# Modulation vectors on GpSimd alone, in buffers of their own, spread over the scans

## The chip, the core and the metric

The kernel runs on one core of one Trainium2 chip. The metric is the device time of one execution in microseconds (us). The engines are called as in the profile: PE (TensorE; PEld is its weight load), DVE (VectorE), ACT (ScalarE), POOL (GpSimd) and SP (SyncE, which issues the DMAs). Each engine works through its own instructions strictly in the order that was fixed when the kernel was built, and semaphores tie the engines together.

## What is computed

One layer of a diffusion backbone over 512 latent tokens and 256 context tokens of width 1024. Cut to what matters here:

```python
m = silu(c) @ w_ada + b_ada            # 1 x 1024 by 1024 x 6144: six vectors of 1024
sh1, sc1, g1, sh2, sc2, g2 = split(m, 6)
h = rms_norm(x) * (1 + sc1) + sh1      # parameters 0 and 1 are needed first
z = h @ w_in
a = bidirectional_gated_deltanet(z)    # 8 heads
b = bidirectional_mlstm(z)             # 4 heads
y = merge(a @ w_a, b @ w_b, gates) @ w_out
x = x + g1 * y                         # parameters 2 to 5 are needed after both mixers
x = x + g2 * conv_ffn(rms_norm(x) * (1 + sc2) + sh2)
```

Both mixers are computed in chunks along the sequence, with a state that goes from chunk to chunk in each direction. For the context tokens a second modulation vector is made with the same weights.

## The kernel before

**Matmuls.** The large products run in float32 split in two parts: a weight block arrives by DMA (`load_split`, line 93), ACT casts it to its high part (line 101), DVE subtracts to get the low part (line 102), and PE forms three products (`mm3`, lines 112 and 113). Names end in `r`, `h` and `l` for raw, high and low: `mwk2r`, `mwk2h`, `mwk2l` are the key weights of mLSTM head 2. There are two raw buffers.

**Order of the work.** `mixers` goes through twelve scans, s = 0 to 11: eight DeltaNet heads and then four mLSTM heads. `drive` advances one scan step by step (16 steps in a DeltaNet head, 12 in an mLSTM head), and after each step it emits pieces of other work: projections for later heads ("bulk", which keep PE busy) and side work, namely the tail of the head before, the merges of the next DeltaNet head, and the modulation blocks. `follow` and `queue_after` only fix the order on an engine; they make nothing wait at run time. What does wait, waits for data or for a buffer to come free.

**DeltaNet tail.** `gdn_tail` makes a factor `fo` (DVE line 1019, then POOL line 1020), and ACT scales the head's output out of the one PSUM bank `po` (line 1023). The next head's scan begins with a PE product that clears this bank (line 956), so it waits for that scaling.

**mLSTM.** `ml_keys` makes weighted keys `mkw` for both directions on POOL (line 1110). The scan's products are at lines 1131 (`mpc`, which reads `mkw`), 1139 and 1141 (`mp`); ACT and DVE form `mn` (1143, 1144). `ml_tail` makes a factor `mfo` on POOL (line 136), and ACT scales the output `mo` with it (1167).

**Modulation blocks.** Parameters 2 to 5 are 32 column blocks n of 128, each in two half blocks of 256 KB of `w_ada`: 64 loads. A half block is multiplied by silu(c) and summed over its four row groups; the two halves' sums are added, and one narrow PE product (`pad`, lines 289 and 311) adds over the partitions. For n < 16 (`ada_block`) this runs in scans 7 and 8, up to six half blocks a step, in slices of a large buffer `gx` and of a rotating buffer, of which parts later hold the mLSTM values; eight of these n are done by DVE (lines 285 and 287), eight by POOL (277 to 281), and the PE product stands right behind the sum. For n >= 16 (`ada_late`) it runs on POOL (297 to 304) in scans 9 to 11, eleven half blocks a scan, with three buffers, sums in a tag `v` of three buffers that other tiles use too, and the PE product stands one pair later.

Of the kernel before, what the change touches and what calls it, by code (L numbers as in the profile page):

```python
# [67 lines left out]
class Kern:  # L68
# [197 lines left out]
    def ada_block(self, n, i):  # L266

        nc = self.nc
        eng = nc.gpsimd if n in ADA_P else nc.vector
        w = self.aw[(2 * n + i) % len(self.aw)].rearrange("p (k c) -> p k c", k=4)  # L270
        c0 = 2048 + P * n
        nc.sync.dma_start(w, self.I["w_ada"][0][512 * i : 512 * i + 512, c0 : c0 + P].rearrange("(k p) c -> p k c", p=P))
        if i == 0:
            self.half = w[:, 0, :]
        a = self.half
        if eng is nc.gpsimd:
            eng.tensor_tensor(w, w, self.sc[:, 4 * i : 4 * i + 4, 0:1].broadcast_to([P, 4, P]), ALU.mult)
            for m in (2, 1):
                eng.tensor_tensor(w[:, 0:m, :], w[:, 0:m, :], w[:, m : 2 * m, :], ALU.add)
            if i:  # L280
# [1 line left out]
        for k in range(4) if eng is nc.vector else ():
            f = self.sc[:, 4 * i + k, 0:1]
            if i == 0 and k == 0:
                eng.tensor_scalar(a, w[:, 0, :], f, None, ALU.mult)
            else:
                eng.scalar_tensor_tensor(a, w[:, k, :], f, a, ALU.mult, ALU.add)
        if i:
            nc.tensor.matmul(self.pad[:, 2 * n : 2 * n + 2], a, self.ones[:, 0:2], start=True, stop=True)

    def ada_late(self, n, i):

        nc, eng = self.nc, self.nc.gpsimd
        w = self.aw[(2 * n + i) % len(self.aw)].rearrange("p (k c) -> p k c", k=4)
        c0 = 2048 + P * n
        nc.sync.dma_start(w, self.I["w_ada"][0][512 * i : 512 * i + 512, c0 : c0 + P].rearrange("(k p) c -> p k c", p=P))
        eng.tensor_tensor(w, w, self.sc[:, 4 * i : 4 * i + 4, 0:1].broadcast_to([P, 4, P]), ALU.mult)  # L297
        eng.tensor_tensor(w[:, 0:2, :], w[:, 0:2, :], w[:, 2:4, :], ALU.add)
        if i == 0:
            self.half = self.tmp.tile([P, P], F32, tag="v", name=f"as{n}", bufs=3)  # L300
            eng.tensor_tensor(self.half, w[:, 0, :], w[:, 1, :], ALU.add)
            return
# [1293 lines left out]
```

## Time and profile before

| what | value |
|---|---|
| time, median of 3 runs | 1369.64 us (1368.8 to 1374.1) |
| the profiled execution: its time, its span | 1371.71 us, 1370.0 us |
| PE busy | 1308.6 us, 96% of the span |
| DVE, ACT, POOL busy | 906.8, 585.1, 492.0 us |
| TensorE clock granted, mean | 0.982 of full speed |
| DMA | 142 MB, mean 104 GB/s |

An engine's busy time says how full it is over the whole span. What a change in one stretch is worth is read from the places where PE stands idle there, and from the granted clock behind them. The scans 7 to 11, of which the change moves work, run from about 573 to 842 us.

### The profile page before, as it was taken

Reading aid. Unit: us, or ns where it says so; the run is one execution under the profiler, and the core shown is the slowest. Engines: PE = TensorE matmul, PEld = TensorE weight load, DVE = VectorE, ACT = ScalarE, POOL = GpSimd, SP = SyncE. Lnnn points to the kernel's source line nnn. Section 1 sums busy time; section 2 is a strip of 40 time slices with the busy share of each in tenths; the row PEclk is TensorE's granted clock in tenths of the full one; section 3 lists DMA queues with packets and bytes.
Section 4 is the critical chain, followed back from the end, with each engine's and each line's share of the span. In section 5 each row is a group of like instructions: output and inputs, shape, how many; then the busy total and the mean of one; then the engine's idle time right before and its main releaser. Section 6 shows DMA issues by size and latency. Waiting matters only on the chain. (4 is left out here: it accounts for less than half of the span.)

```text
span 1370.0 us, 24204 instructions
## 1 busy us (share of the span) xinstructions
PE 1308.6 (96%) x9436; PEld 1103.6 (81%) x9436; DVE 906.8 (66%) x1863; ACT 585.1 (43%) x1279; POOL 492.0 (36%) x620
## 2 busy tenths in 40 slices
PE   6979999999999999998899989999899999999997
PEld 5867788888888888988798877888697888888885
DVE  5776677957758664654746466453758879979833
ACT  5554664646655654332334335232333433333331
POOL 3323221033130332337546460000344555655452
PEclk9989999999999999999999999999999999999999
DMA  9433333322242233446334331466223323333331
GB/s 284 125 95 82 86 95 91 83 76 74 56 104 75 57 84 106 123 110 182 94 85 116 108 100 54 139 185 202 68 86 94 93 79 107 95 99 100 92 92 62
DMA packets 233233, 141.86 MB, mean 104 GB/s; under 512 B 32977, under 2 KB 215518, under 8 KB 233118
## 3 DMA queue, kind: packets, MB, share of 16 engines
q1 hardware_dynamic: 230958, 140.09, 36.7%
q8 instruction: 74, 1.21, 0.4%
q10 hardware_dynamic: 2160, 0.23, 0.1%
q14 instruction: 41, 0.34, 0.1%
HBM read 134.47 MB, written 5.82 MB: 102 GB/s over the span
## 5 line engine op out<-in xcount | busy, mean ns | idle before, releaser
L1566 DVE SCALAR_TENSOR_TENSOR y<-pu,fw,y 128x441 f32<-128x441 f32 (+2 forms) x352 | 230.0, 691 | 39.2 <-ACT y L1557 33.6
L136 POOL TENSOR_TENSOR rs<-pw_t,mhalf 128x1 f32<-128x1 f32 x14 | 8.1, 580 | 171.5 <-DVE pw_t L135 171.5
L884 POOL TENSOR_TENSOR qs<-qs,qT 128x512 f32<-128x512 f32 x16 | 23.2, 1452 | 78.2 <-DMA qs<-gd 62.0
L297 POOL TENSOR_TENSOR aw<-aw,sc 128x512 f32<-128x512 f32 x32 | 38.8, 1219 | 31.7 <-DMA aw<-in_w_ada_dram 31.6
L136 POOL TENSOR_TENSOR kh<-pw_t,phalf 128x6 f32<-128x6 f32 x8 | 10.9, 1358 | 104.2 <-DVE pw_t L135 61.9
L832 POOL MEMSET gx<- 96x16 f32 x8 | 1.0, 124 | 121.3 <-DMA gx<-scr 121.3
L986 ACT ACTIVATE v<-p,sc 128x128 f32<-128x128 f32 x80 | 25.4, 370 | 36.5 <-PE p L978 36.4
L1557 ACT ACTIVATE y<-pu,fw 128x512 f32<-128x512 f32 x44 | 30.1, 684 | 20.2 <-PE pu L113 12.6
L839 POOL TENSOR_TENSOR gx<-gx,iv_t 96x14 f32<-96x14 f32 (+6 forms) x112 | 35.1, 314 | 8.7
L1135 DVE SCALAR_TENSOR_TENSOR C<-C,ge,mpc 128x257 f32<-128x257 f32 x32 | 15.4, 480 | 32.8 <-PE mpc L1131 32.5
L837 POOL TENSOR_TENSOR iv_t<-gx 96x14 f32<-96x14 f32 (+6 forms) x112 | 33.5, 299 | 8.0
L647 ACT ACTIVATE cv_t<-cv_y 128x512 f32<-128x512 f32 (+1 forms) x40 | 21.8, 545 | 32.3 <-DVE cv_y L646 31.4
L1340 DVE SCALAR_TENSOR_TENSOR x<-x,py 128x512 f32<-128x512 f32 x16 | 11.0, 687 | 36.9 <-PE py L113 36.9
L1508 POOL TENSOR_TENSOR al<-y,ah 128x512 fp32r<-128x512 f32 x22 | 28.9, 1311 | 14.7 <-ACT ah L1507 13.2
L974 DVE SCALAR_TENSOR_TENSOR X<-p,colA,vt 128x128 f32<-128x128 f32 x80 | 23.9, 338 | 12.5 <-PE p L970 12.2
L698 DVE SCALAR_TENSOR_TENSOR Eg<-Eg,colA,mask 128x128 f32<-128x128 f32 x96 | 30.6, 387 | 1.7 <-DMA Eg<-gd 1.7
L1518 DVE TENSOR_TENSOR fd_t<-pd,m 128x512 f32<-128x512 f32 x8 | 5.3, 684 | 37.2 <-PE pd L113 37.2
L1003 ACT ACTIVATE v<-p,sc 128x128 f32<-128x128 f32 x64 | 23.1, 379 | 13.9 <-PE p L990 10.9
L1506 DVE TENSOR_TENSOR y<-y,y 128x512 f32<-128x512 f32 x22 | 28.1, 1277 | 0.9
L990 PE MATMUL p<-v,kt 128*128 128x128 f32 x160 | 25.9, 284 | 2.4 <-ACT v L986 2.4
L970 PE MATMUL p<-S,kT 128*128 128x128 f32 x160 | 27.6, 287 | 0.4 <-DVE S L995 0.2
L990 PEld LDWEIGHTS p<-v,kt 128*128 128x128 f32 x160 | 22.2, 190 | 7.0 <-ACT v L986 5.8
(1234 smaller groups left out, 4611.2 us busy)
## 6 DMA issues: line engine op xcount, KB each, us to landing
aw<-in_w_ada_dram SPq DMA_DIRECT2D x41, 256.0 KB
uw<-in_w_ada_dram SPq DMA_DIRECT2D x16, 512.0 KB
Eg<-gd SPq DMA_DIRECT2D x16, 384.0 KB
gx<-in_w_ada_dram SPq DMA_DIRECT2D x23, 256.0 KB
qs<-gd SPq DMA_DIRECT2D x16, 256.0 KB
xn<-in_x_dram SPq DMA_DIRECT2D x4, 512.0 KB
Em<-r1d SPq DMA_DIRECT2D x8, 256.0 KB
mwo_0r<-in_w_in_dram SPq DMA_DIRECT2D x4, 512.0 KB
```

What stands on the lines that cost most here:

```text
L297: eng.tensor_tensor(w, w, self.sc[:, 4 * i : 4 * i + 4, 0:1].broadcast_to([P, 4, P]), ALU.mult)
L698: self.follow(nc.vector.scalar_tensor_tensor(E[:, c, :], E[:, c, :], self.colA[:, c, d, row : row + 1], self.mask[d], ALU.add, ALU.min), "v")
L837: eng.tensor_tensor(t, Bi[:, 0:j, j : j + 1].broadcast_to([8 * NB, j, n]), Bi[:, j : j + 1, j + 1 :].broadcast_to([8 * NB, j, n]), ALU.mult)
L839: g = eng.tensor_tensor(Bi[:, 0:j, j + 1 :], Bi[:, 0:j, j + 1 :], t, ALU.add)
L970: g = nc.tensor.matmul(p1[:, d, :], kT[:, c * P : c * P + P], S[d], start=True, stop=True)
L974: self.anchor["v"] = nc.vector.scalar_tensor_tensor(X[d], p1[:, d, :], self.colA[:, c, 2 + d, h : h + 1], vt[:, c, :], ALU.mult, ALU.subtract)
L986: self.anchor["s"] = nc.scalar.activation(v3[d], p2[:, d, :], AF.Copy, scale=sc[d][:, 2 + j, c : c + 1])
L990: g = nc.tensor.matmul(p3[:, d, :], kt[:, c, :], v3[d], start=True, stop=True)
L1506: nc.vector.tensor_tensor(ys[0], ys[0], ys[1], ALU.mult)
L1508: nc.gpsimd.tensor_tensor(al[:, j, :], ys[0], ah[:, j, :].bitcast(F32), ALU.subtract)
L1557: nc.scalar.activation(y, ps, AF.Copy, scale=tap(0, 0))
L1566: g = nc.vector.scalar_tensor_tensor(o, u3[:, r0 + dy : r1 + dy, c0 + dx : c1 + dx], tap(dy, dx), o, ALU.mult, ALU.add)
```

## The change

All 64 half blocks go through one generator, `ada_late`, on POOL. Loads have a tag of their own, `aw`, with two buffers: the load of block j + 1 is issued before the work on block j, and has to wait for the buffer of block j - 1. The sums have a tag of their own, `as`, with eight buffers. The generator is advanced by one block a step from scan 5 on, with the numbers of blocks per scan in `ADA`; the PE products come only when the bank `pad` exists (scan 7), up to two a block, at least one pair behind. The first direction's weighted keys alternate between two buffers, and the second direction's have a tag `kw` with one buffer (before, they shared a tag with decay rows). In `ml_tail` the scaling of `mo` comes one piece later and is ordered behind the last `mn` on ACT. The scratch area for dynamic DMAs in SBUF is made smaller (`dynamic_dma_scratch_size=2048`).

```diff
-ADA = 6
-ADA_P = (0, 4, 7, 8, 10, 12, 14, 15)
+ADA = (0, 0, 0, 0, 0, 4, 12, 14, 12, 12, 10, 0)
...
+    def ada_late(self):
+        nc, eng = self.nc, self.nc.gpsimd
+        def load(j):
+            w = self.hold.tile([P, 4, P], F32, tag="aw", name=f"aw{j}", bufs=2)
+            i, c0 = j % 2, 2048 + P * (j // 2)
+            self.follow(nc.sync.dma_start(w, self.I["w_ada"][0][512 * i : 512 * i + 512, c0 : c0 + P].rearrange("(k p) c -> p k c", p=P)))
+            return w
+        w = load(0)
+        for j in range(64):
+            nxt = load(j + 1) if j < 63 else None
+            self.follow(eng.tensor_tensor(w, w, self.sc[:, 4 * (j % 2) : 4 * (j % 2) + 4, 0:1].broadcast_to([P, 4, P]), ALU.mult))
+            eng.tensor_tensor(w[:, 0:2, :], w[:, 0:2, :], w[:, 2:4, :], ALU.add)
+            if j % 2 == 0:
+                a = self.hold.tile([P, P], F32, tag="as", name=f"as{j}", bufs=8)
+                eng.tensor_tensor(a, w[:, 0, :], w[:, 1, :], ALU.add)
+            else:
+                eng.tensor_tensor(w[:, 0, :], w[:, 0, :], w[:, 1, :], ALU.add)
                 eng.tensor_tensor(a, a, w[:, 0, :], ALU.add)
+                self.sums.append((j // 2, a))
+            for _ in range(2):
+                if self.pad is not None and len(self.sums) > 1:
+                    self.ada_sum()
+            w = nxt
+            yield
...
-            k_ = self.rot.tile([P, NCH, P], F32, tag=("Dm", "E")[d], name=f"mkw{h}_{d}", bufs=1 + d)
+            k_ = self.rot.tile([P, NCH, P], F32, tag=("kw" if d else ("Dm", "kv")[h % 2]), name=f"mkw{h}_{d}")
...
-            nc.scalar.activation(o[c], o[c], AF.Copy, scale=f[:, c : c + 1])
-        yield 0.0
+            self.follow(nc.scalar.activation(o[c], o[c], AF.Copy, scale=f[:, c : c + 1]), "s")
...
-            if s in (GH - 1, GH):
-                side.append((self.some(s - GH + 1), range(100)))
-            if s > GH:
-                side.append((islice(self.ada, 11), range(100)))
+            side.append((islice(ada, ADA[s]), range(100)))
```

The orders below are those in which each engine issues its instructions. On DVE, in the first mLSTM scan (s = 8), before the change, with the low part of the key weights of head 2 (`mwk2l`) among the modulation operations:

```order
843 L1019 SCALAR_TENSOR_TENSOR fo_8279<-sso_8270,ssq_6775 128x4
844 L287 SCALAR_TENSOR_TENSOR aw<-aw,sc 128x128 x3
845 L285 TENSOR_SCALAR aw<-aw,sc 128x128
846 L287 SCALAR_TENSOR_TENSOR aw<-aw,sc 128x128 x3
847 L1133 COPY C_8199<-mpc_8200 128x257
848 L287 SCALAR_TENSOR_TENSOR aw<-aw,sc 128x128 x2
849 L102 TENSOR_TENSOR mwk2l<-mwk2r,mwk2h 128x1024
850 L287 SCALAR_TENSOR_TENSOR aw<-aw,sc 128x128
```

and after it:

```order
827 L1003 SCALAR_TENSOR_TENSOR fo_8364<-sso_8355,ssq_6801 128x4
828 L1115 COPY C_8310<-mpc_8311 128x257
829 L101 TENSOR_TENSOR mwk2l<-mwk2r,mwk2h 128x1024
830 L1115 COPY C_8310<-mpc_8352 128x257
831 L101 TENSOR_TENSOR mwq2l<-mwq2r,mwq2h 128x1024
```

The modulation operations are gone from DVE, and the low part stands right behind the copy of the state.

On POOL, at the end of scan 4, where the factor `fo` of a DeltaNet tail is made, before the change:

```order
267 L839 TENSOR_TENSOR gx<-gx,iv_t 96x14
268 L884 TENSOR_TENSOR qs_1_5725<-qs_1_5725,qT_4635 128x512
269 L884 TENSOR_TENSOR qs_0_6501<-qs_0_6501,qT_5448 128x512
270 L1020 TENSOR_TENSOR fo_6062<-fo_6062,mhalf 128x4
```

and after it, with the first modulation blocks:

```order
267 L823 TENSOR_TENSOR gx<-gx,iv_t 96x14
268 L278 TENSOR_TENSOR aw_6026<-aw_6026,sc 128x512
269 L868 TENSOR_TENSOR qs_1_5725<-qs_1_5725,qT_4635 128x512
270 L279 TENSOR_TENSOR aw_6026<-aw_6026 128x256
271 L278 TENSOR_TENSOR aw_6028<-aw_6028,sc 128x512
272 L282 TENSOR_TENSOR as_6032<-aw_6026 128x128
273 L868 TENSOR_TENSOR qs_0_6527<-qs_0_6527,qT_5448 128x512
274 L1004 TENSOR_TENSOR fo_6070<-fo_6070,mhalf 128x4
```

Four modulation operations have come to stand ahead of `fo`.

On POOL again, where the second direction's weighted keys of mLSTM head 1 are made (`mkw_1`, end of scan 8), before the change:

```order
401 L1110 TENSOR_TENSOR mkw_0_8803<-mkt_7952,colB 128x768
402 L1089 MEMSET va_8643 128x1 x6
403 L1110 TENSOR_TENSOR mkw_1_8805<-mkt_7952,colB 128x768
404 L136 TENSOR_TENSOR mfo_8865<-pw_t,mhalf 128x4
405 L301 TENSOR_TENSOR as_9031<-aw_8815 128x128
```

and after it, where `aw_8625` and `aw_8663` are the two halves of one column block and `as_8667` is their sum:

```order
464 L278 TENSOR_TENSOR aw_8625<-aw_8625,sc 128x512
465 L1092 TENSOR_TENSOR mkw_1_8910<-mkt_8050,colB 128x768
466 L279 TENSOR_TENSOR aw_8625<-aw_8625 128x256
467 L278 TENSOR_TENSOR aw_8663<-aw_8663,sc 128x512
468 L282 TENSOR_TENSOR as_8667<-aw_8625 128x128
469 L279 TENSOR_TENSOR aw_8663<-aw_8663 128x256
470 L284 TENSOR_TENSOR aw_8663<-aw_8663 128x128
471 L285 TENSOR_TENSOR as_8667<-as_8667,aw_8663 128x128
```

The keys, which have to wait for the buffer that head 0 still reads, now stand inside a modulation block, and the rest of that pair stands behind them. The PE product that reads `as_8667` directly follows the first PE product that reads `mkw_1_8910`.

## Rows read from the trace of the kernel before

**Rows 1.** The page, its first part: busy time, share of the span and instructions of each engine.
```profile
PE 1308.6 (96%) x9436; PEld 1103.6 (81%) x9436; DVE 906.8 (66%) x1863; ACT 585.1 (43%) x1279; POOL 492.0 (36%) x620
```

**Rows 2.** Timeline of PE: start, duration (both us), instruction; in brackets idle before it and releaser.
```profile
461.59 0.38 PE L956 MATMUL po<-zero 128*128 128x512 bf16 x1 [0.17 <-ACT o L1023]
...
578.33 0.38 PE L113 MATMUL pc_mk<-hc,mwk1l 128*128 128x256 f32 x1 [1.41 <-DVE mwk1l L102]
...
631.86 0.70 PE L1131 MATMUL mpc<-gx,mkw 128*128 128x257 f32 x2 [0.82 <-ACT o L1023]
...
640.04 0.52 PE L113 MATMUL pc_mk<-hc,mwk2l 128*128 128x256 f32 x1 [3.30 <-DVE mwk2l L102]
...
657.18 0.70 PE L1141 MATMUL mp<-gx,mp 128*128 128x257 f32 x2 [1.87 <-DVE mn L1144]
...
676.50 0.38 PE L289 MATMUL pad<-ones,aw 128*128 128x2 f32 x2 [2.24 <-POOL aw L281]
677.15 0.70 PE L1131 MATMUL mpc<-gx,mkw 128*128 128x257 f32 x2
...
687.04 0.28 PE L112 MATMUL pv<-mwv_1h,hc 128*128 128x256 f32 x1
...
791.63 0.70 PE L1131 MATMUL mpc<-va_cg,mkw 128*128 128x257 f32 x2 [0.89 <-POOL mkw L1110]
...
811.36 1.23 PE L1139 MATMUL mp<-C,mqT 128*128 128x257 f32 x2 [2.58 <-ACT mn L1143]
```

**Rows 3.** Windows: length, busy us (instructions) of each engine, granted clock, DMA share, GB/s.
```profile
640.00:644.00 4.00, 3.96 (x20) 3.96 (x21) 2.66 (x4) 0.00 (x0) 3.81 (x6) 0.57 0.77 200
676.50:682.00 5.50, 5.47 (x18) 4.42 (x19) 2.01 (x8) 0.48 (x1) 2.10 (x9) 0.69 0.25 56
811.30:816.00 4.70, 4.64 (x18) 3.90 (x19) 2.62 (x8) 1.38 (x5) 4.36 (x7) 0.69 0.09 27
```

**Rows 4.** Timeline of DVE in the first mLSTM scan.
```profile
636.60 1.72 DVE L287 SCALAR_TENSOR_TENSOR aw<-aw,sc 128x128 f32<-128x128 f32 x2 [1.32 <-DMA aw<-in_w_ada_dram]
638.25 1.74 DVE L102 TENSOR_TENSOR mwk2l<-mwk2r,mwk2h 128x1024 fp32r<-128x1024 f32 x1
```

**Rows 5.** Timeline of ACT, two places.
```profile
634.13 1.05 ACT L101 CAST mwk2h<-mwk2r 128x1024 fp32r<-128x1024 f32 x1 [1.79 <-PE pv L113]
...
809.24 1.70 ACT L1167 ACTIVATE mo<-mo,mfo 128x256 f32<-128x256 f32 x4 [5.06 <-POOL mfo L136]
```

**Rows 6.** Groups on POOL, 460 to 860 us: busy us, mean ns, idle before and releaser.
```profile
L297 POOL TENSOR_TENSOR aw<-aw,sc 128x512 f32<-128x512 f32 x32 | 38.8, 1219 | 31.7 <-DMA aw<-in_w_ada_dram 31.6
L298 POOL TENSOR_TENSOR aw<-aw 128x256 f32<-128x256 f32 x32 | 25.5, 807 | 0.2
L1110 POOL TENSOR_TENSOR mkw<-mkt,colB 128x768 f32<-128x768 f32 x8 | 12.9, 1611 | 33.4 <-DVE mp L1082 21.7 <-DVE mkt L1073 11.7
L301 POOL TENSOR_TENSOR as<-aw 128x128 f32<-128x128 f32 x16 | 9.3, 586 | 28.0 <-PE pad L311 28.0
```

**Rows 7.** Timeline of SP: issues of two loads.
```profile
605.85 0.37 SPq L93 DMA_DIRECT2D mwk2r<-in_w_in_dram  x1
...
656.82 0.46 SPq L296 DMA_DIRECT2D aw<-in_w_ada_dram  x1
```

**Rows 8.** Waits of SP: total us, times, longest us.
```profile
SPq L296 <- POOL as L301: 61.0, 12, 13.0
```

**Rows 9.** Timeline of POOL, two places.
```profile
458.06 1.29 POOL L884 TENSOR_TENSOR qs<-qs,qT 128x512 f32<-128x512 f32 x1 [1.96 <-DMA qs<-gd]
459.31 1.06 POOL L1020 TENSOR_TENSOR fo<-fo,mhalf 128x4 f32<-128x4 f32 x1
...
661.06 1.05 POOL L297 TENSOR_TENSOR aw<-aw,sc 128x512 f32<-128x512 f32 x1 [3.15 <-DMA aw<-in_w_ada_dram]
```

**Rows 10.** Instructions of line 102 on DVE, 400 to 540 us: min/median/max ns.
```profile
L102 DVE TENSOR_TENSOR wk7l<-wk7r,wk7h x1: 1226/1226/1226, 439.9 to 439.9; 128x1024 fp32r<-128x1024 f32 x1
```

**Rows 11.** The same line on DVE, 680 to 860 us.
```profile
L102 DVE TENSOR_TENSOR wg_3l<-wg_3r,wg_3h x2: 1501/1798/2095, 764.5 to 771.0; 128x1024 fp32r<-128x1024 f32 x2
```

More of the change, by code (lines that the diff above doesn't have):

```diff
@@ L264, in ada_cols @@
         nc.vector.scalar_tensor_tensor(self.modA[:, k, :], self.mod[:, KC + k, :], 1.0, self.n1w[:, k : k + 1].broadcast_to([P, 2]), ALU.add, ALU.mult)
[L266 to L280, printed above, removed]
-                eng.tensor_tensor(a, a, w[:, 0, :], ALU.add)
[L282 to L302, printed above, removed]
-        eng.tensor_tensor(w[:, 0, :], w[:, 0, :], w[:, 1, :], ALU.add)
-        eng.tensor_tensor(self.half, self.half, w[:, 0, :], ALU.add)
-        self.sums.append((n, self.half))
-        if len(self.sums) > 1:
-            self.ada_sum()
+    def ada_late(self):
[15 more added lines that the diff above has]
+                eng.tensor_tensor(w[:, 0, :], w[:, 0, :], w[:, 1, :], ALU.add)
+                eng.tensor_tensor(a, a, w[:, 0, :], ALU.add)
+                self.sums.append((j // 2, a))
[4 more added lines that the diff above has]
+            yield
@@ L1035, in ml_values @@
         n = MDV + 1
-        while h in (1, 2) and self.ada_n < 16 * h:
-            next(self.ada)
         if h < 2:
@@ L1165, in ml_tail @@
         self.rpow(f, ss, 1.0 / MDV, EPS, self.mhalf)
+        yield 0.0
         for c in range(XC):
-            nc.scalar.activation(o[c], o[c], AF.Copy, scale=f[:, c : c + 1])
-        yield 0.0
+            self.follow(nc.scalar.activation(o[c], o[c], AF.Copy, scale=f[:, c : c + 1]), "s")
         yield 0.0
@@ L1198, in drive @@
                 pass
-    def ada_all(self):
-        for j in range(2):
-            t = self.gx[:, G1 : 2 * G1] if j == 0 else self.rot.tile([P, G1], F32, tag="Bx", name="aw")
-            self.aw = [self.gx[:, 2 * G1 + 512 * i : 2 * G1 + 512 * i + 512] for i in range(2)]
-            self.aw += [t[:, 512 * i : 512 * i + 512] for i in range(3)]
-            for n in range(8 * j, 8 * j + 8):
-                for i in range(2):
-                    self.ada_block(n, i)
-                    self.ada_n = 2 * n + i + 1
-                    yield
-        self.aw = [self.hold.tile([P, NT], F32, tag="qs", name=f"aw{i}", bufs=3) for i in range(3)]
-        for n in range(16, 32):
-            for i in range(2):
-                self.ada_late(n, i)
-                self.ada_n = 2 * n + i + 1
-                yield
     def mixers(self, e_hc, l1):
@@ L1220, in mixers @@
         self.st, self.qs, self.po = {}, {}, {}
-        self.ada_n, self.sums = 0, []
+        self.pad, self.sums = None, []
         self.chain, self.bi = {}, None
@@ L1236, in mixers @@
         tail = nothing
+        ada = self.ada_late()
         for s in range(GH + MH):
@@ L1277, in row_tiles @@
         return (self.rot.tile([P, P], F32, tag=f"S{i}", name=f"mrow{i}", bufs=2)[: (P, 16)[i], : (16, P)[i]] for i in range(2))
-    def some(self, j):
-        while self.ada_n < 16 * (j + 1):
-            for _ in range(ADA):
-                if self.ada_n < 16 * (j + 1):
-                    next(self.ada)
-            yield
     def early_gates(self, n):
@@ L1582 @@
     from concourse.bass_utils import run_bass_kernel_spmd as _run
-    nc = _bacc.Bacc("TRN2", target_bir_lowering=False, num_devices=1)
+    nc = _bacc.Bacc("TRN2", target_bir_lowering=False, num_devices=1, dynamic_dma_scratch_size=2048)
     arrays, args = {}, {}
```

3 lines of the change are left out of this document (1 added, 2 removed).

## The prediction

> **What bounds the kernel now.** I first read the busy times: PE is busy 1308.6 us of a span of 1370.0, and the next engine, DVE, 906.8 [rows 1]. The reader is to see that only time in which PE stands still, or runs at a lower clock, can be won, and that the change adds no PE work and takes none away. I then went through PE's timeline for the stretch that the change touches, the end of the DeltaNet heads and the mLSTM heads, and kept the stops that its work can reach. From 575 us on there are seven [rows 2]: 1.41 us before 578.33 (for `mwk1l` from DVE), 0.82 before 631.86 (for the scaling of `o` on ACT), 3.30 before 640.04 (for `mwk2l` from DVE), 1.87 before 657.18 (for `mn` from DVE), 2.24 before 676.50 (for a modulation sum from POOL), 0.89 before 791.63 (for `mkw` from POOL) and 2.58 before 811.36 (for `mn` from ACT). Together that is 13.1 us. Last I read the granted clock behind the three longest. After the stop of 3.30 it is 0.57 over 4.0 us, after the one of 2.24 it is 0.69 over 5.5 us, after the one of 2.58 it is 0.69 over 4.7 us, a mixture of full speed, 2.4 GHz, and half, 1.2 GHz; PE is busy all the while [rows 3]. What full speed would have saved there is 4.0 x 0.43 + 5.5 x 0.31 + 4.7 x 0.31 = 1.7 + 1.7 + 1.5 = 4.9 us.
>
> **What the change removes.** Take the stops in turn.
>
> *DVE's share of the modulation work.* `mwk2h` is cast on ACT from 634.13 to 635.18 [rows 5], but its low part starts on DVE only at 638.25, because two modulation operations stand ahead of it and one of them waits 1.32 us for its load [rows 4]. In the new order nothing but a copy stands there, so `mwk2l` can start at about 635.3 and end by 636.6 to 637.0. PE fell idle at 640.04 - 3.30 = 636.74. I take 3.1 of 3.30 us. At 578.33 the same low part would be gated by its own cast; I take 1.2 of 1.41. At 631.86 the scaling of `o` waits for `fo`, which on DVE stands behind four modulation operations (the order shows three more after it); I take all of 0.8. At 657.18 `mn` stands between modulation operations on DVE; all of 1.87 goes.
>
> *The PE product right behind its sum.* The stop before 676.50 is of this kind. Now the product stands at least a pair later: 2.24 us.
>
> *POOL late in the scans.* Before 791.63 POOL makes `mkw` among sums, in one buffer; a second buffer lets it be made earlier: 0.89 us. Before 811.36 ACT stands 5.06 us for `mfo` from POOL [rows 5], and the `mn` that PE needs is behind that scaling. By then POOL has no modulation block left, since `ADA` gives the last in scan 10: 2.58 us. In the new order the scaling still stands between the two `mn`, so the move of it in `ml_tail` by itself is worth nothing here; the free POOL is.
>
> Sum of the stops: 1.2 + 0.8 + 3.1 + 1.87 + 2.24 + 0.89 + 2.58 = 12.7 us. With the clock behind three of them, 4.9 us, it is 17.6 us.
>
> **What it adds.** *POOL's work.* A pair of half blocks is two multiplications of 1.22 us, two additions of 0.81 and three small ones of at most 0.59 [rows 6]: 5.8 us. Eight pairs come over from DVE, 47 us. POOL is busy 36% of the span, so this fits; the question is when each sum is ready. With two buffers, a load is issued when the block before the present one is done. A load behind a weight load takes from its issue at 656.82 [rows 7] to 661.06 [rows 9], 4.2 us. Then a pair needs 4.2 + 2.9 = 7.1 us. From 578.33 to 631.86 [rows 2] there are 14 blocks to do, seven pairs: 50 us of 53.5. From 640.04 to 687.04, twelve blocks, 43 us of 47. It fits, with 4 us to spare a scan, and the sixteen blocks of scans 5 and 6 have no PE product waiting for them until scan 7.
>
> *Where it is tight.* The second direction's keys of head 1 now wait until head 0's last read of that buffer, the product at 677.15 to 677.85. Behind them stands the rest of a pair: 1.61 + 0.81 + 1.22 + 0.59 + 0.81 + 0.59 + 0.59 = 6.2 us, and up to 1.8 more if the second half's load is a slow one: 6.2 to 8.0. PE comes to the product that reads this sum just ahead of 687.04, 9.2 us later, or 7.5 without the 1.7 us at lower clock. The margin lies between +1.3 and -0.5 us. Two or three places in the four scans are like it. I take 2 us for all of them, 0 at best and 6 at worst (three stops of 2 us; a longer one would bring the lower clock back).
>
> *The DeltaNet tails.* `fo` at 459.31 now has four modulation operations ahead of it: 1.22 + 0.81 + 1.22 + 0.59 = 3.8 us. The operation ahead of it had waited 1.96 us for its load [rows 9], so `fo` comes 1.9 us later at most. PE's clearing of the bank already waited 0.17 us for the scaling behind `fo` [rows 2], so it has no slack. I take 1.5 us there and 0.5 in the tail after it, together 2.0; 0.5 at best (operations shorter than their means), 5 at worst (a load that lands late and is waited for).
>
> *DVE and POOL together.* In the stretch before the modulation work, a low part on DVE takes 1226 ns [rows 10]; among modulation operations on POOL, 1501 to 2095 ns for the same shape [rows 11]. POOL's work is now spread over more of the span. I take 1.0 us on the path, 0 to 3. The Trainium skill, SBUF — State Buffer, section "SBUF: two separate sides", says that VectorE and GpSimd have one pair of SBUF ports that goes as a whole to whichever starts first, when VectorE reads two SBUF inputs. The longer times agree with this; by that rule alone each low part that meets a multiplication on POOL would be late by up to that operation, and ten of them would take up to 12 us from the sum, where the measured rows make it 6 (the second rival below).
>
> The smaller scratch area and the sums' own tags cost nothing by themselves; what they hide is POOL's wait of 28.0 us for `pad` [rows 6], off PE's path.
>
> **The sum.** 17.6 - 2.0 - 2.0 - 1.0 = 12.6 us less. Against the profiled execution, 1371.71 us, that gives 1359.1; this execution lies 2.1 us above the median of 1369.64, so for a median I forecast 1357.0. Bounds: all gains and the least costs, 17.6 - 0.5 = 17.1, 1352.5; gains without the clock and the worst costs, 12.7 - 14 = -1.3, 1371.
>
> **The rivals.**
>
> *1. The waits move to the sums.* PE's products for `pad` stand at fixed places in its order. If three of them catch POOL late, by 2.5 us each, the clock drops again behind each, as it did after 2.24 us [rows 3]: 3 x (2.5 + 1.6) = 12.3 us against 17.6 - 3.0 = 14.6. Time: 1367, no change. For it: the margin above is near nothing. Against it: a pair's 7.1 us fits the scans' pace.
>
> *2. The ports eat part of it.* If POOL and DVE stretch each other as [rows 11] against [rows 10] show, by 0.3 to 0.9 us, on each of some ten low parts and `mn` additions that PE waits for, that is 6 us more: 1363. For it: those rows. Against it: before the change DVE itself did eight pairs beside POOL in the same scans, and this share of the meetings goes away.
>
> *3. Slower, by SP's order.* SP issues one load after the other. A modulation load that waits for its buffer holds up the weight loads behind it; before the change this happened with a longest hold of 13.0 us [rows 8]. With two buffers instead of five and three, and POOL itself waiting for PE in `mkw`, holds can grow. Point of decision: `mwk2r` is issued at 605.85 [rows 7] and cast at 634.13, 28 us later; with 4 us for the load, a hold of 24 us is free. At 35 us the weights are 11 us late, and with one such hold in each of three heads that is 33 us against 17.6: 1369.6 + 15 = 1385. Against it: nothing in the new orders makes POOL wait that long with a weight load behind.
>
> *4. All of it comes, or more:* 1352 or less.
>
> **How the numbers follow.** The forecast, 1352 to 1362, has 0.58; rival 1 has 0.17, rival 2 0.10, rival 3 0.10, rival 4 0.05. Half a per cent, 6.8 us, is about what a measurement of this kernel tells from no change, so faster means below 1362.8 us. Faster: 0.58 + 0.05 and a third of rival 2, 0.66. Slower: 0.10 and a little of rival 1, 0.11. The rest, 0.23, is no change. The range of 8 in 10 goes from 1351.5 to 1368: it takes in the forecast, rival 2 and the better part of rival 1, and leaves out rival 3 and a gain beyond the sum.
>
> **What would show it.** On PE's timeline, the stops for `mwk2l`, `mn` and `mfo` are gone, and the granted clock stays at 1.00 through the stretches of 4.0, 5.5 and 4.7 us. New stops, if any, stand before the clearing of `po` in scans 5 and 6 (1 to 2 us) and before `pad` products. The prediction is wrong if `pad` products wait over 2 us each, if a weight load's cast is waited for by PE, or if DVE's low parts grow to 2 us where PE needs them.

## The result and the profile after

The changed kernel takes 1363.03 us (median of 12 runs, 1358.92 to 1367.66) where the kernel before takes 1369.5 (12 runs, 1366.77 to 1374.1): a ratio of 0.995, with a 95% interval of 0.9936 to 0.9963. It is faster by about 6.5 us, half of the 12.6 that were forecast. The profiled execution has a time of 1361.81 us and a span of 1360.1. The page's first part answers to [rows 1]:

```profile
PE 1305.4 (96%) x9436; PEld 1102.8 (81%) x9436; DVE 891.1 (66%) x1799; ACT 584.1 (43%) x1279; POOL 532.8 (39%) x676
```

POOL took over 40.8 us of work and DVE lost 15.7. What PE waited for from head 4 to the end of the scans (window 404 to 832 us; total us, times, longest):

```profile
PE po L940 <- ACT o L1007: 5.2, 2, 3.7
...
PE pv L111 <- ACT gx L1083: 1.3, 1, 1.3
```

Apart from one of 2.9 us before `py`, the first product behind the scans, no other stop in this list is longer than 0.6 us. None of the seven stops of [rows 2] from 575 us on is left. In their place stand three others, two of them before the clearing of `po` (line 940 now, 956 before) and one before `pv`, the value products of mLSTM head 1. The wait before `py` stands in the kernel before too, with 2.91 us. The same places on PE's timeline (start, duration, instruction; in brackets idle before it and releaser), with the clearings for heads 4, 5, 6 and 7:

```profile
404.05 0.39 PE L940 MATMUL po<-zero 128*128 128x512 bf16 x1
...
461.95 0.58 PE L940 MATMUL po<-zero 128*128 128x512 bf16 x1 [3.71 <-ACT o L1007]
...
523.18 0.38 PE L940 MATMUL po<-zero 128*128 128x512 bf16 x1 [1.49 <-ACT o L1007]
...
576.10 0.38 PE L940 MATMUL po<-zero 128*128 128x512 bf16 x1
...
630.15 0.38 PE L111 MATMUL pv<-mwv_0h,hx 128*128 128x256 f32 x1 [1.32 <-ACT gx L1083]
...
831.79 0.50 PE L111 MATMUL py<-oh,wb_1h 128*128 128x512 f32 x1 [2.90 <-ACT oh L1273]
```

The granted clock behind the three stops, in windows (length, busy us and instructions of PE, PEld, DVE, ACT and POOL, granted clock, DMA share, GB/s):

```profile
461.60:468.00 6.40, 6.05 (x17) 4.78 (x17) 3.48 (x9) 4.17 (x10) 2.86 (x4) 0.52 0.27 80
523.00:530.00 7.00, 6.82 (x124) 5.46 (x124) 3.46 (x7) 2.87 (x7) 3.15 (x8) 1.00 0.42 109
630.00:636.50 6.50, 5.88 (x34) 5.67 (x35) 0.39 (x2) 3.86 (x17) 1.94 (x2) 0.74 0.00 0
640.00:831.00 191.00, 188.15 (x1051) 164.35 (x1049) 107.90 (x242) 72.87 (x153) 101.73 (x123) 1.00 0.39 104
```

Behind 461.95 it is 0.52, nearly the lower level of 1.2 GHz all through, and PE is busy: 6.4 x 0.48 = 3.1 us are lost. In the two further profiles of this kernel (below) it is 0.72 over 6.2 us and 0.74 over 6.0 there, 1.7 and 1.6 us. Behind 630.15 it is 0.74: 6.5 x 0.26 = 1.7 us. From 640 on, where [rows 3] had 0.57 and twice 0.69, it stays at 1.00, 2.4 GHz.

For a sum by stage I take the starts of three PE instructions: the clearing for head 4, the one for head 7, and the first `py` product. In the kernel before they are

```profile
408.58 0.39 PE L956 MATMUL po<-zero 128*128 128x512 bf16 x1
...
572.77 0.38 PE L956 MATMUL po<-zero 128*128 128x512 bf16 x1
...
842.48 0.79 PE L112 MATMUL py<-oh,wb_1h 128*128 128x512 f32 x1 [2.91 <-ACT oh L1320]
```

| kernel | scans 4 to 6 | scans 7 to 11 | sum |
|---|---|---|---|
| before | 164.2 | 269.7 | 433.9 |
| changed | 172.1 | 255.7 | 427.7 |

Scans 7 to 11 gave back 14.0 us, and scans 4 to 6 took 7.9 of it. The stops and the clock account for both, nearly. In scans 7 to 11 the stops of before, with two small ones of 0.2 that the list left out, were 13.5 us and the lower clock behind them 4.9, together 18.4. After, they are 1.32 + 0.48 (a product just behind it) and three small ones of 1.3 together, with 1.7 of clock: 4.8. The difference is 13.6 of the measured 14.0. In scans 4 to 6 the stops at the clearings are 3.71 + 1.49 against 0.17 before, the smaller ones 1.2 against 0.6, and the clock 3.1, together 8.7 for the measured 7.9. The starts for head 4, 408.58 and 404.05, lie in work that the change doesn't touch, so 4 us of a difference between two whole spans can be noise from there. The stretch is the better measure, and even for it three profiles of the changed kernel gave 423.5, 427.1 and 427.7.

**Why the scaling of `o` was late.** ACT at the stop of 3.71 us and at the one of 1.32:

```profile
460.03 0.84 ACT L683 ACTIVATE Eg<-Eg 128x768 f32<-128x768 f32 x1 [6.67 <-DVE Eg L682]
460.78 1.12 ACT L1007 ACTIVATE o<-po,fo 128x128 f32<-128x128 f32 x4
...
629.21 0.63 ACT L683 ACTIVATE Em<-Em 128x512 f32<-128x512 f32 x1 [7.68 <-DVE Em L682]
629.74 0.35 ACT L1083 COPY gx<-pv 128x256 f32<-128x256 f32 x1
```

The scaling stands behind the exponential of `Eg`, head 7's decay rows, and that had waited 6.67 us for DVE. Both late evictions of the timeline have this form: an ACT instruction that PE needs stands behind an exponential that nobody needs yet. In the kernel before, ACT has the scaling first:

```profile
460.40 1.14 ACT L1023 ACTIVATE o<-po,fo 128x128 f32<-128x128 f32 x4 [2.94 <-POOL fo L1020]
461.42 0.85 ACT L699 ACTIVATE Eg<-Eg 128x768 f32<-128x768 f32 x1
```

So the change has turned ACT's order round at this place. `fo` itself was there 4 us earlier, by POOL's timeline, which shows the second stop's story too:

```profile
450.08 1.04 POOL L278 TENSOR_TENSOR aw<-aw,sc 128x512 f32<-128x512 f32 x1
451.08 1.29 POOL L868 TENSOR_TENSOR qs<-qs,qT 128x512 f32<-128x512 f32 x1
452.32 0.73 POOL L279 TENSOR_TENSOR aw<-aw 128x256 f32<-128x256 f32 x1
453.01 1.05 POOL L278 TENSOR_TENSOR aw<-aw,sc 128x512 f32<-128x512 f32 x1
454.01 0.46 POOL L282 TENSOR_TENSOR as<-aw 128x128 f32<-128x128 f32 x1
454.43 1.28 POOL L868 TENSOR_TENSOR qs<-qs,qT 128x512 f32<-128x512 f32 x1
455.88 1.01 POOL L1004 TENSOR_TENSOR fo<-fo,mhalf 128x4 f32<-128x4 f32 x1 [0.17 <-DVE fo L1003]
...
518.69 1.29 POOL L868 TENSOR_TENSOR qs<-qs,qT 128x512 f32<-128x512 f32 x1 [3.75 <-DMA qs<-gd]
519.94 1.04 POOL L278 TENSOR_TENSOR aw<-aw,sc 128x512 f32<-128x512 f32 x1
520.94 1.02 POOL L1004 TENSOR_TENSOR fo<-fo,mhalf 128x4 f32<-128x4 f32 x1
```

At the second stop `qs` waits 3.75 us for its load, a modulation multiplication of 1.04 us follows, and only then comes `fo`: 1.49 us. Why the exponential was late at the first stop is seen on DVE, in `ssq` (the sums of squares that `fo` needs), in `fo` and in the instructions of the row weights `Eg` (min/median/max ns):

```profile
451.43 4.31 DVE L783 TENSOR_SCALAR ssq<-ssq 128x4 f32<-128x4 f32 x1
455.65 0.15 DVE L1003 SCALAR_TENSOR_TENSOR fo<-sso,ssq 128x4 f32<-128x4 f32 x1
...
L682 DVE SCALAR_TENSOR_TENSOR Eg<-Eg,colA,mask x12: 335/439/1125, 456.2 to 461.6; 128x128 f32<-128x128 f32 x12
```

and in the kernel before, at the same place:

```profile
455.53 0.60 DVE L799 TENSOR_SCALAR ssq<-ssq 128x4 f32<-128x4 f32 x1
457.20 0.16 DVE L1019 SCALAR_TENSOR_TENSOR fo<-sso,ssq 128x4 f32<-128x4 f32 x1 [1.08 <-ACT junk L1017]
...
L698 DVE SCALAR_TENSOR_TENSOR Eg<-Eg,colA,mask x12: 334/336/1433, 457.8 to 462.2; 128x128 f32<-128x128 f32 x12
```

`ssq`, 128x4 in size, takes 4.31 us where it took 0.60; for most of the other heads it is 0.17. It ends at 455.74, with the unbroken row of six POOL operations that ends at 455.71; four of the six are modulation work. One of the row weights takes 335 ns alone, with a median of 336 before. Now half of them take 439 or more, while POOL works on modulation blocks; the longest is no sign of the change, since the kernel before has one of 1433 ns, beside POOL's `qs`. From the start of `ssq` to the end of the twelve rows it is 10.54 us, 6.98 before. Of the 3.56 more, 2.55 have come about by the start of `fo` and 1.01 behind it; in the first repetition below it is 1.32 and 1.75. So `ssq` and the row weights both make the exponential late.

The rows of `Em`, the mLSTM heads' decay rows, come late by a load:

```profile
620.13 1.27 DVE L1064 TENSOR_TENSOR mp<-mpqk,Em 128x512 f32<-128x512 f32 x2
...
628.03 2.19 DVE L682 SCALAR_TENSOR_TENSOR Em<-Em,colA,mask 128x128 f32<-128x128 f32 x8 [4.74 <-DMA Em<-r1d]
```

SP issued that load at 621.97 us. The former rows in the buffers were read last by the two products at 620.13, which end at 620.81 and 621.40, so SP's order can have delayed the load by 1.2 us at most. From its issue to the first row it took 6.06 us. In the eight profiles, of this kernel and of versions below, in which POOL has all the modulation work and this order and these buffers stand, that time is 4.91 to 7.10 us, and the stop before `pv` grows with it, from 0.3 to 0.5 us at 4.9 to 2.2 us at 7.0 to 7.1. What stretches the load isn't shown.

The theory is therefore: the gains came as forecast; what was lost is DVE's `ssq` and row weights, held and stretched by POOL's work, or late by a load, and ACT's fixed order, which puts the exponential of these rows ahead of an eviction that PE waits for. The rivals: ACT's order alone is to blame (then turning it round gives the 3.7 us and the clock back); `fo` is late on POOL, as the prediction had it (then the stops go when POOL does nothing in scan 5); the shared buffers of the weighted keys; and, on the gains' side, that DVE's relief brought nothing and only pace and buffers did.

### The profile page after: what moved, and what is told of

Same layout as the page of the kernel before. It is cut to its first block, busy times and chain, and to the rows that moved or that the text cites. A ratio compares the mean times of both kernels' runs of the same rounds, so it can differ in the third digit from the quotient of the medians.

```text
span 1360.1 us, 24176 instructions
## 1 busy us (share of the span) xinstructions
PE 1305.4 (96%) x9436; PEld 1102.8 (81%) x9436; DVE 891.1 (66%) x1799; ACT 584.1 (43%) x1279; POOL 532.8 (39%) x676
## 5 line engine op out<-in xcount | busy, mean ns | idle before, releaser
L278 POOL TENSOR_TENSOR aw<-aw,sc 128x512 f32<-128x512 f32 x64 | 69.2, 1084 | 65.2 <-DMA aw<-in_w_ada_dram 65.2
L279 POOL TENSOR_TENSOR aw<-aw 128x256 f32<-128x256 f32 x64 | 53.8, 843 | 3.1
L970 ACT ACTIVATE v<-p,sc 128x128 f32<-128x128 f32 x80 | 25.4, 369 | 35.6 <-PE p L962 35.6
L981 DVE SCALAR_TENSOR_TENSOR S<-S,ge,p 128x128 f32<-128x128 f32 x64 | 19.1, 339 | 15.9 <-PE p L974 15.4
L1125 ACT ACTIVATE mn<-mp,colA 128x257 f32<-128x257 f32 x32 | 15.1, 473 | 32.6 <-PE mp L1121 30.3
```

The costliest lines, as they stand in the source:

```text
L278: self.follow(eng.tensor_tensor(w, w, self.sc[:, 4 * (j % 2) : 4 * (j % 2) + 4, 0:1].broadcast_to([P, 4, P]), ALU.mult))
L970: self.anchor["s"] = nc.scalar.activation(v3[d], p2[:, d, :], AF.Copy, scale=sc[d][:, 2 + j, c : c + 1])
```

## The experiments

"Ratio" is against the kernel before in the same set of runs. Sums are of the stretch of the table above, from one profile each, made before rounding.

**The changed kernel again, twice.** No edit.

> The changed kernel once more, beside the experiments on the same chip. Both theories: 0.995 of the kernel before (0.993 to 0.997), with PE's stop of about 3.7 us before the clearing of the bank po at the start of scan 5 and one of about 1.3 us before a product of the values of mLSTM head 1 (pv<-mwv_0h).

Measured: 1361.1 us (6 runs), ratio 0.9926 [0.9901, 0.9951]; 169.4 + 257.7 = 427.1. The stop stood there again, with 3.5 us; `ssq` took 3.07 us and the twelve `Eg` instructions had a median of 536 ns. Besides the 1.32 us before `pv` there was a second stop of this kind, of 1.50, at 697 us.

> The changed kernel beside e9 and e10 on the same chip: 0.993 to 0.996 of the kernel before, 427 to 428 us from the clearing of po for head 4 to the first product of py.

Measured: 1364.12 us, ratio 0.995 [0.9936, 0.9965]; 170.2 + 253.4 = 423.5. The stop before the clearing was 3.71 us and `ssq` 4.31, but the stop before `pv` only 0.58. So one profile's sum is good to some 4 us, and scans 4 to 6 are 169.4 to 172.1 every time, against 164.2 before.

**ACT scales `o` ahead of the exponential of `Eg`.**

```diff
-            nc.scalar.activation(o[:, c, :], po[:, c, :], ...)
+            self.last_o = nc.scalar.activation(o[:, c, :], po[:, c, :], ...)
...
-        nc.scalar.activation(E..., AF.Exp)
+        self.queue_after(nc.scalar.activation(E..., AF.Exp), self.last_o if row == GH - 1 else None)
```

> One ACT instruction is moved: the exponential of the first decay rows of head 7 (Eg) stands behind the scaling of o of head 4 instead of ahead of it, and nothing else that bears on the time. Theory A (the lost part of the gain is this order: ACT holds o back behind an exponential that waits for DVE): the stop of 3.7 us falls to 0.5 or less, the 2.9 us lost at half clock behind it go too, 1357 us, 0.990 to 0.992 of the kernel before. Rival (the prediction's own step: fo itself is late on POOL behind four modulation operations): the stop stays over 1.5 us and the time within 2 us of the changed kernel.

Measured: 1363.54 us, ratio 0.9936 [0.991, 0.9961]; 168.6 + 254.3 = 422.9. The time is that of the changed kernel. PE's timeline shows a stop at the next product,

```profile
467.66 0.75 PE L974 MATMUL p<-v,kt 128*128 128x128 f32 x4 [2.67 <-ACT v L970]
```

and ACT's timeline shows why:

```profile
463.42 1.14 ACT L1007 ACTIVATE o<-po,fo 128x128 f32<-128x128 f32 x4 [3.90 <-POOL fo L1004]
...
466.51 0.84 ACT L683 ACTIVATE Eg<-Eg 128x768 f32<-128x768 f32 x1 [1.95 <-DVE Eg L682]
467.26 0.61 ACT L970 ACTIVATE v<-p,sc 128x128 f32<-128x128 f32 x2
```

The exponential waits for DVE where it stands, and now `v` is behind it. `ssq` takes 3.49 us here. The stop is some 1 us shorter than the one it replaces and the clock stays at 1.00 behind it, but scans 4 to 6 are only 1 to 4 us shorter than in the changed kernel and 4.4 above the 164.2 of before. The order decides who waits, not that somebody waits. The rival "order alone" falls at this place.

**No modulation block in scan 5.**

```diff
-ADA = (0, 0, 0, 0, 0, 4, 12, 14, 12, 12, 10, 0)
+ADA = (0, 0, 0, 0, 0, 0, 14, 14, 12, 12, 12, 0)
```

> No modulation block in scan 5: ADA is (0,0,0,0,0,0,14,14,12,12,12,0). Theory A: the old ACT order (scaling first) comes back by itself, the stop at the start of scan 5 falls to the 0.2 us of before, and 5 to 6.5 us are won; the stop of 1.5 us at the start of scan 6 may go or stay, since the blocks of scan 6 start there: 1356 to 1358 us. Rival (the pace of scans 5 and 6 is needed so that the sums are ready later): new stops before pad products in scan 7, 1363 us or more.

Measured: 1367.64 us, ratio 0.9974 [0.9956, 0.9993]; 170.0 + 256.3 = 426.3 in a profile whose execution took 1360.93 and was the fastest of its 12. ACT has the scaling of `o` first again here, as in the kernel before, and the stop at 461.95 had shrunk to 0.38 us, but the clearings of heads 6 and 7 waited 1.8 and 2.34 us. For head 6, POOL has `qs`, a modulation multiplication of 1.05 us and then `fo`, as at the second stop of the changed kernel. For head 7 no modulation work stands between `qs` and `fo`; there `qs` itself had waited 3.55 us, by the profile for a product of `pv`. So blocks at the start of scan 6 cost PE there as those of scan 5 did; the stop of head 7 isn't shown to be theirs. Why its other runs took 7 us more isn't settled: no profile shows one.

**The second direction's keys in the decay rows' buffers, as before.**

```diff
-tag=("kw" if d else ("Dm", "kv")[h % 2])
+tag=("E" if d else ("Dm", "kv")[h % 2]), bufs=1 + d
```

> The second direction's weighted keys go back to the tag of the decay rows, so the second decay row of mLSTM heads 2 and 3 is again loaded late. Theory B (PE's stop of 1.3 us before pv<-mwv_0h, and the half clock behind it, come from SP holding the decay rows' load behind modulation loads that wait for their two buffers): the stop stays, time within 2 us of the changed kernel. Rival (the stop comes from the second decay row being made early, ahead of the eviction on ACT): the stop goes and 3 us are won, 1360 us.

Measured: 1364.16 us, ratio 0.9953 [0.9937, 0.9969]; 169.6 + 256.7 = 426.3. What PE waited for in it:

```profile
PE po L940 <- ACT o L1007: 4.0, 2, 3.2
PE mpqk L1059 <- DVE mkt L1055: 2.6, 4, 1.4
```

The stop before `pv` is gone, since the rows of `Em` come at another time, and others stand in its place, the longest of 1.35 us (in the list) and of 1.33 before a product of the modulation rows. The shared buffers neither cause the loss nor can be told from the buffers of their own by the time.

**Blocks begin later in scans 5, 6 and 7** (step 8, 4 and 2).

```diff
-            side.append((islice(ada, ADA[s]), range(100)))
+            side.append((islice(ada, ADA[s]), range({5: 8, 6: 4, 7: 2}.get(s, 0), 100)))
```

> Same numbers of blocks per scan, but in scans 5, 6 and 7 the blocks start only at step 8, 4 and 2, so that none stands ahead of fo on POOL or beside the decay rows of head 7 on DVE. Measured in the profile from the clearing of po for head 4 to the first product of py (before 433.9 us, changed 427.8 and 427.1 us, of them scans 4 to 6 164.2 against 172.0 and 169.4). Theory A2 (the loss is POOL's new work at the tails: DVE's decay rows take 0.54 to 1.13 us beside it instead of 0.34, and fo comes late): scans 4 to 6 take 164 to 166 us, the whole stretch 420 to 422 us, 0.989 of the kernel before. Rival (the blocks that start later make the sums late for their PE products in scan 7): scans 7 to 11 take 260 us or more and the whole stays at 426 to 429 us.

Measured: 1361.88 us, ratio 0.9927 [0.9902, 0.9953]; 165.4 + 259.5 = 424.8. Scans 4 to 6 are nearly back at the 164.2 of before. Scans 7 to 11 are not better: the load of `Em` took 7.10 us to its first row, and PE waited 2.2 us before `pv` and 1.3 for `v` next to it, with a clock of 0.74 over 13 us. `ssq` is back at 0.29 us. ACT has the scaling of `o` first here too; so it is in every version below that begins its blocks later.

**Scan 5 without the multiplications.** The multiplication and the first addition of the first four blocks are left out, so their part of the modulation vectors isn't computed. Loads and small sums stay.

```diff
+            if j > 3:
                 self.follow(eng.tensor_tensor(w, w, ..., ALU.mult))
                 eng.tensor_tensor(w[:, 0:2, :], w[:, 0:2, :], w[:, 2:4, :], ALU.add)
```

> The changed kernel without the multiplication and the first addition of the first four blocks (their sums are left wrong), loads and small additions as before. Theory A2: DVE's ten operations on the decay rows of head 7 take 0.34 us each again, and the stop at the start of scan 5 falls to under 1 us. Rival (loads on the DMA rings or SP's order make them late): the operations stay at 0.5 to 1.1 us or start late, and the stop stays over 2.5 us.

Measured: one run, 1361.0 us; 166.0 + 255.1 = 421.1. The `Eg` instructions, and ACT's order:

```profile
L683 DVE SCALAR_TENSOR_TENSOR Eg<-Eg,colA,mask x12: 338/342/1359, 460.0 to 465.0; 128x128 f32<-128x128 f32 x12
...
463.21 1.14 ACT L1008 ACTIVATE o<-po,fo 128x128 f32<-128x128 f32 x4 [3.53 <-POOL fo L1005]
464.23 0.86 ACT L684 ACTIVATE Eg<-Eg 128x768 f32<-128x768 f32 x1
```

`ssq` takes 0.50 us instead of 4.31, the median of the rows is 342 ns instead of 439 and 536, and from the start of `ssq` to the end of the rows it is 7.60 us instead of 10.54. The stop before the clearing is 0.76 us instead of 3.5 and 3.7. But the edit has also turned ACT's order back to that of before, so the fall from 3.7 to 0.76 isn't POOL's alone. The second experiment has the same order with the multiplications: there PE stops 2.67 us for `v`, here 0.76 before the clearing and 0.62 for `v` (0.17 and 0.61 in the kernel before), and scans 4 to 6 take 168.6 there and 166.0 here. With the order equal, POOL's large operations are what holds `ssq`, stretches the rows and keeps PE waiting.

**The kernel before, with all modulation blocks on POOL.** This is DVE's relief alone, at the old pace and with the old buffers.

```diff
-ADA_P = (0, 4, 7, 8, 10, 12, 14, 15)
+ADA_P = tuple(range(16))
```

> The kernel before with one thing changed: all sixteen n of the first part on POOL, in the old buffers and at the old pace. Theory (DVE's relief is what removes the stops for mwk1l, o, mwk2l and mn): these four stops, 7.4 us, are gone; scans 7 to 11, 269.7 us before and 255.7 and 257.7 in the changed kernel, take 259 to 263 us, the rest of the gain being that of the sums' lag and of mfo. Rival (the old pace of six half blocks a step overloads POOL instead): new stops before pad products and for fo on POOL, 268 us or more.

Measured: one run, 1376.64 us; 164.6 + 275.6 = 440.2, which is 6.3 us more than before in the stretch. The kernel before in the same set had a median of 1373.22 us (12 runs, 1365.87 to 1376.64), so the time is not faster, and no more than that is shown. What PE waited for:

```profile
PE pad L289 <- POOL gx L281: 5.5, 5, 2.4
PE pv L112 <- ACT mwv_1h L101: 3.5, 2, 3.2
...
PE pc_mk L113 <- DVE mwk2l L102: 1.2, 1, 1.2
PE pc_mk L113 <- DVE mwk1l L102: 0.9, 1, 0.9
```

The low part of head 2's keys is waited for 1.2 us instead of 3.30 [rows 2], that of head 1 for 0.9 instead of 1.41, and the stops for `o` and `mn` are gone: 5.3 of the 7.4 us, so the relief does most of what the prediction said. But POOL, six half blocks a step, is late for the product right behind the sum, five times and up to 2.4 us. The wait of 3.2 for `mwv_1h` has the form seen above: its weights were issued 20 us earlier, but the cast stands on ACT behind an exponential of `Em` that waits 5.08 us for DVE.

**The changed kernel, with DVE's eight n of before back on DVE.** For n < 16 and not in (0, 4, 7, 8, 10, 12, 14, 15):

```diff
+                for k in range(4):
+                    f = self.sc[:, 4 * (j % 2) + k, 0:1]
+                    if j % 2 == 0 and k == 0:
+                        self.follow(nc.vector.tensor_scalar(a, w[:, 0, :], f, None, ALU.mult))
+                    else:
+                        nc.vector.scalar_tensor_tensor(a, w[:, k, :], f, a, ALU.mult, ALU.add)
```

> The changed kernel with the same eight n given back to DVE, in the new buffers and at the new pace. Theory (DVE's relief): stops for low parts or mn on DVE come back in scans 7 and 8, scans 7 to 11 take 260 us or more. Rival (own buffers and the even pace are enough, whoever does the work): 255 to 258 us, and scans 4 to 6 shorter than in the changed kernel, since POOL has less work at the tails.

Measured: one run, 1365.67 us; 173.5 + 257.1 = 430.6. That is 3 to 7 us above the three profiles of the changed kernel, and below the 433.9 of before. None of the seven stops of before is back; the longest are 3.83 us for a state copy and 2.11 for `mkt`, both from DVE. At the new pace DVE's share is done by 618 us, ahead of the first mLSTM scan. One run of each is little to go by; the experiment comes again below on a better ground.

**Blocks begin later in scans 5 and 6 only** (step 8 and 4), scan 7 as in the change.

```diff
+            side.append((islice(ada, ADA[s]), range({5: 8, 6: 4}.get(s, 0), 100)))
```

> As e5, but scan 7 starts its blocks at step 0 again (scan 5 at 8, scan 6 at 4). Theory A2: scans 4 to 6 take 164 to 166 us as in e5, scans 7 to 11 255 to 258 us as in the changed kernel, together 420 to 423 us against 433.9 before and 427.1 to 427.8 changed; 0.990 of the kernel before. Rival (blocks that come later in scans 5 and 6 push the decay rows of scan 7 late, whatever scan 7 does): scans 7 to 11 take 259 us or more, as in e5.

Measured: 1357.8 us, ratio 0.9903 [0.9888, 0.9917]; 164.8 + 255.8 = 420.6. The interval lies below that of the changed kernel in the same set, [0.9936, 0.9965]. Scans 4 to 6 stand at 164.8, and scans 7 to 11 where they were.

**The same, and ACT's exponentials of the `Em` rows of heads 2 and 3 ordered behind the evictions of `pv`.**

```diff
-                (nc.scalar.copy, nc.vector.tensor_copy)[VA[i]](va[c + i]..., ps...)
+                self.last_v = (nc.scalar.copy, nc.vector.tensor_copy)[VA[i]](va[c + i]..., ps...)
...
+        self.queue_after(nc.scalar.activation(E..., AF.Exp), self.last_v if row >= GH + 2 else None)
```

> As e9, and on ACT the exponentials of the decay rows of mLSTM heads 2 and 3 stand behind the evictions of the values of the head before. Theory B2 (PE's stop before pv<-mwv_0h comes from an eviction that stands behind such an exponential, which waits for DVE and the load): that stop, 1.3 to 2.2 us, and the half clock behind it go, scans 7 to 11 take 252 to 254 us, the whole 417 to 420 us, 0.987 of the kernel before. Rival (the rows are needed early, or the evictions wait for something else): the stop stays or another comes at mp or mpqk, 255 us or more.

Measured: 1352.38 us (4 runs, 1350.53 to 1354.82), ratio 0.9867 [0.985, 0.9884]; 165.0 + 251.4 = 416.4. This version is faster than both kernels. What PE waited for in it:

```profile
PE py L111 <- ACT oh L1273: 2.9, 1, 2.9
...
PE p L974 <- ACT v L970: 0.6, 1, 0.6
```

Apart from `py`, which all have, no stop is longer than 0.6 us. The granted clock at the two places, which was 0.52 and 0.74 in the changed kernel:

```profile
458.00:468.00 10.00, 8.99 (x151) 7.12 (x150) 6.74 (x15) 5.60 (x12) 0.00 (x0) 1.00 0.36 91
620.00:640.00 20.00, 19.97 (x150) 18.84 (x149) 6.21 (x14) 8.16 (x23) 11.22 (x19) 1.00 0.42 111
```

`ssq` takes 0.17 us here, and the median of the `Eg` rows is 342 ns. Here the order on ACT did help, where that of `Eg` had only moved a wait: no new stop stands behind the exponential of `Em`.

**The last version, with DVE's eight n back on DVE.** The edit is that of the eighth experiment, on the tenth.

> As e10, but the same eight n as before the change are DVE's again, in the new buffers and at e10's pace. Theory C (the gain of scans 7 to 11 comes from the pace and the buffers, not from who does the work): scans 7 to 11 take 251 to 254 us, and the whole from head 4 to py 416 to 421 us, 0.987 to 0.990 of the kernel before. Rival (DVE has to be free of the work, as the prediction argued): low parts or mn or the state copies come late on DVE again, scans 7 to 11 or 4 to 6 take 3 us or more longer than in e10, 420 us or more, 0.991 or slower.

Measured: 1360.26 us, ratio 0.9925 [0.9901, 0.9949]; 166.7 + 255.8 = 422.4. What PE waited for:

```profile
PE mpqk L1070 <- DVE mkt L1066: 2.1, 1, 2.1
PE po L951 <- ACT o L1018: 2.1, 3, 1.1
```

Without DVE's relief 7.9 us of the time (1360.26 - 1352.38, from two sets in which the kernel before had 1371.1 and 1371.17) and 6.0 of the stretch are gone, with a long wait for DVE (`mkt`), behind which the clock is 0.75 over 6.3 us. The intervals don't touch. None of the seven stops of before is back here either: DVE's share runs from 486 to 614 us.

## Why the prediction was half right

The measured median lies in the range that was given 8 chances in 10, 1351.5 to 1368, and outside the forecast of 1352 to 1362. The 6.5 us are just under the 6.8 from which the prediction speaks of faster, though the interval is clear of no change. That the time lies in the range is in part luck: the gains came in the size that was forecast, but the costs were 17.6 less the 6.2 to 10.4 us won in the stretch, 7 to 11 us instead of 5.0, and the largest had another cause than the one it was given.

**What the change removes: right, 17.6 us.** All seven stops went, 13.1 us together, and the clock stands at 1.00 where it had 0.57 and 0.69. The tenth experiment, which has the whole change and hardly a new stop, is 17.5 us below before in the stretch and 18.8 in time (1371.17 - 1352.38). That is the sum of the gains in size. That it meets 17.6 so closely is chance: one profile's sum is good to some 4 us, this version has edits of its own and small stops of 0.4 to 0.6 us, and it loses two small ones that the prediction left out.

**DVE's relief: right only together with the new pace.** The prediction gave four of the seven stops to work that leaves DVE. Alone the relief took 5.3 us of these 7.4 away, but brought no time, since POOL at six blocks a step was late. Pace, buffers and orders without the relief gave 433.9 - 422.4 = 11.5 of the 17.5 us, and the relief the last 6.0. With DVE's share back at the new pace none of the four stops returned, since the share now lies ahead of the first mLSTM scan; the 6.0 us come from waits in scans 4 to 7 that the prediction didn't name. So what removed the four stops is that the work left their place on DVE; the two runs with DVE's share back show that the spreading over earlier scans is enough for that.

**The DeltaNet tails: the step that failed.** The prediction had `fo` behind four modulation operations on POOL and 2.0 us for both tails, 5 at worst. The place was right, the first tail's cause was not, and the size was wrong: three profiles have 7.9, 5.2 and 6.0 us more in scans 4 to 6. At 461.95 `fo` was 4 us early; the scaling stood on ACT behind an exponential that waited for DVE, in an order that the change had turned round, and 3.1 us of clock (1.7 and 1.6 in the repetitions) came behind the 3.71 of the stop. The term had no clock in it. At 523.18 the step was right in kind: `fo` did stand behind modulation work, 1.04 of the 1.49 us, and the rest goes with `qs`, late by its load.

**DVE and POOL together: under-sized, and with ACT's order the cause of the first.** The term had 1.0 us, 0 to 3, from low parts in the mLSTM scans. It should have gone to `ssq` and the twelve row weights of `Eg`: 2.55 and 1.01 us on the way to the exponential, 1.32 and 1.75 in the repetition. Most of the loss in scans 4 to 6 goes with POOL's work at their starts, as the experiment without multiplications (166.0) and the later start (165.4, 164.8) show beside the turned order alone (168.6). The Trainium skill, SBUF — State Buffer, section "SBUF: two separate sides", has VectorE and GpSimd block each other for a whole instruction when VectorE reads two SBUF inputs. The trace agrees for the row weights: they read two, and their 0.335 us grow by up to 0.79 beside modulation work, and by 1.10 before beside `qs`, less than that multiplication's 1.29 us on POOL. `ssq` reads one and was held through several POOL operations, which that sentence doesn't cover. The second rival, which said that this would eat 6 us and the time be 1363, named the right price and result, but put it on the low parts and on `mn`, none of which PE waited for over 0.52 us.

**The rows of `Em`: not foreseen.** The stop of 1.32 us before `pv`, with 0.48 next to it and 1.7 us of clock, comes from a load that took 6.06 us and from ACT's order. It has no term in the sum. Turning its order round gave 1357.8 - 1352.38 = 5.4 us, and 255.8 - 251.4 = 4.4 in the scans. The ninth experiment's own waits for evictions of this kind were 1.5 us there, and 0.5 for `v`; so some 2 us of it are shown to come from the order. Waits of 0.80 for a sum and 0.26 for a low part are gone too, and the rest lies within what one profile tells.

**Where it is tight: over-sized.** The term had 2.0 us for products that catch POOL late. The changed kernel has none in two of its three profiles and one of 0.52 in the third; its variants have up to 0.80. The first rival, three stops of 2.5 us, falls: no `pad` product waited over 0.8 us for a sum from POOL at the new pace, only at the old one (2.4).

**SP's order: the third rival falls.** SP's waits for modulation buffers in the changed kernel, 404 to 832 us:

```profile
SPq L272 <- POOL as L282: 82.9, 21, 12.7
```

The longest is 12.7 us, against 13.0 in [rows 8], and far below the 24 us that were free. (The total can't be set beside the 61.0 there, since the kernel before had further waits for modulation buffers.) PE waited for no weight's cast. The load that did come late was a small one, `Em`'s, and SP's part in that is 1.2 us at most.

What stays open: the spread of the kernel without blocks in scan 5, what stretches the load of `Em`, why `ssq` is held so long, how much of the first stop is ACT's order and how much DVE's lateness, and what the later scaling in `ml_tail` is worth by itself, which wasn't tried. A third load buffer for the modulation blocks wasn't tried either.

## What to carry to other kernels

When work is moved to an idle engine, look not only at what stands behind it there, but also at who shares its time: short VectorE instructions ahead of an exponential were the tightest chain here, and beside an unbroken row of GpSimd operations one of 0.17 us took 4.31. Compare the orders on all engines, not only on the two that swap work: here the third, ACT, had two instructions turned round. On an in-order engine, search for an instruction that waits for something not yet needed and has an eviction for PE behind it; turning the two round pays only if what then comes behind it isn't needed either. Start background work in a part of the loop in which no such chain runs, here eight steps later, before you spend a buffer on it.
